# A hybrid decoder layer on one core: low parts of weights shared with GpSimd, recurrence products spread over four array quadrants

## The chip, the core and the metric

The kernel runs on one core of one Trainium2 chip. The metric is the device time of one execution in microseconds (us). Every engine named here belongs to that core: TensorE (PE in the profile; PEld is its weight load), VectorE (DVE), ScalarE (ACT), GpSimd (POOL) and SyncE (SP), whose queue issues most of the DMA transfers.

## What is computed

One layer of a decoder on 264 tokens at once: 256 tokens of a prompt and one new token for each of 8 other sequences. The model width is 2048. The parts are:

```python
x = x + 0.5 * swiglu(rmsnorm(x, n1), f1g, f1u, f1d)      # first FFN, inner width 5504
h = rmsnorm(x, nm)
proj = h @ w_in                                          # 2048 x 4864
# attention: 16 query heads, 4 key/value heads, window 128, sinks, relative bias
# RWKV-7 time mixing, 16 heads of 64x64 state:
#   S = S * exp(logw) + (S @ -kk) (kk * a)^T + v k^T ;  y = S @ r
x = x + concat(o_att, o_rwkv) @ w_out
x = x + 0.5 * swiglu(rmsnorm(x, n2), f2g, f2u, f2d)      # second FFN
```

All inputs and outputs are float32. The outputs are the final norm of x, new key/value windows, the recurrence's states and the last projected columns ("shift").

## The kernel before, in words

**Weights.** Every large product is made in three passes of a reduced float32 format (`F32R`). `chunk` (line 125) loads 128x512 weights into `raw` by a DMA on SP, ScalarE rounds them into `hi` (line 132), and another engine subtracts, `lo = raw - hi` (the helper `tt`, line 59). `gemm` (line 136) takes 16 such 128x128 blocks in chunks of four, and for each block issues three matmuls of 264 columns: `hi*xh`, `hi*xl`, `lo*xh`. There are 6 buffers of `raw` and 4 of `hi` and of `lo`, so that ScalarE can round at most about three chunks ahead of the one that TensorE reads. `chunk` runs with high priority: the scheduler may put it ahead of other work of its engines. The engine for `lo` is VectorE everywhere.

**Stages.** The first FFN, then `mixing_body` (w_in, attention, recurrence, w_out), then the second FFN. In the mixing stage `win(t)` (line 399) computes one of 38 tiles of 128 columns of `proj` (4 chunks, 48 matmuls): tiles 0 and 1 are the small projections, 2 to 25 belong to the eight pairs of recurrent heads (three tiles each), 26 to 29 to keys and values, 30 to 37 to queries. `SEQ` (line 39) has their order. After each chunk `gemm` calls `tick`, which advances every waiting task (a Python generator) to its next `yield`. So the small work of the recurrence and of attention lies between large matmuls, and `pause(n)` moves a step by n chunks. A list scheduler then writes the order of each engine, and each engine runs its order strictly.

**Recurrence.** The tasks take the head pairs in four batches of two. `prep` (one for each pair) builds, from the projected tiles, decays, keys and 64x64 matrices for four time blocks of 64 tokens (`c`); it ends with `gv` (line 524, products of `Gm` and `UV`) and `dps` (line 530, the eight other sequences' states times two vectors, 64x64 by 64x2). `chain` (one for each batch) reloads 32x32 blocks in another layout, runs a 30-step triangular solve on VectorE (lines 570 to 577, tiles `st` and `Xt`), completes the inverse `TT` with 32x32 products, and then makes, for both pairs and four blocks: `wus` (line 614, `TT` by two of the three parts of `KR`, 64x128), copies of it into `W` and `uv` by ScalarE and VectorE in turn (lines 622 and 626), `pbs` (lines 628 to 637: `W` by `BT` and `W` by `Gm`), `pN` and `pY`, and then three steps over `c` (line 660) that carry the state `S`: each multiplies `PT` by `S` into one bank and `S` by `KR` into `pY`. A 64x64 product reads one half of the 128 partitions (`HALF`) and writes one half. In all these products but `gv` the half written is the half read, so that the two heads of a pair use two of the four quadrants of TensorE's array.

After the last `prep`s the shift output `shc` is sent by a DMA on ScalarE's queue (line 887, right after the last batch is started); `shc` is filled by one small GpSimd copy for each tile (line 412). At the end of the last chain five transposes of `XD` (line 701) and ScalarE's copies (lines 703, 704) make `XR` for the states of the 8 other sequences, which are finished in the second FFN. Eight-column copies `y<-XD` stand on ScalarE (line 680).

Of the kernel before, what the change touches and what calls it, by code (L numbers as in the profile page):

```python
# [10 lines left out]
ALU = mybir.AluOpType  # L11
AX = mybir.AxisListType

P = 128
# [33 lines left out]
def body(tc, I, O):  # L48
# [51 lines left out]
    with ExitStack() as ctx:  # L100
# [24 lines left out]
        def chunk(src, n, e, ahead=True):  # L125
            w = n * P
            with tc.high_priority() if ahead else nullcontext():
                raw = wp.tile([P, CH * P], F32, tag="raw", bufs=NRAW, name=uid("raw"))
                hi = wp.tile([P, CH * P], F32R, tag="hi", bufs=NHL, name=uid("hi"))
                lo = wp.tile([P, CH * P], F32R, tag="lo", bufs=NHL, name=uid("lo"))  # L130
                SP.dma_start(raw[:, :w], src)
                A.copy(hi[:, :w], raw[:, :w])  # L132
                tt(e, lo[:, :w], raw[:, :w], hi[:, :w].bitcast(F32), ALU.subtract)
            return hi, lo

        def gemm(ps, src, xs, step=None, rng=None, ahead=True, ready=None):
            n = len(xs)
            for k0 in range(0, n, CH):
                k1 = min(n, k0 + CH)
                if rng and k0 not in rng:  # L140
                    continue
                hi, lo = ready or chunk(src[:, k0 * P:k1 * P], k1 - k0, V, ahead)
                for k in range(k0, k1):
                    xh, xl = xs[k]
                    c = slice((k - k0) * P, (k - k0 + 1) * P)
                    mm(ps[:, :T], hi[:, c], xh, k == 0, False)
                    mm(ps[:, :T], hi[:, c], xl, False, False)
                    big[0] = mm(ps[:, :T], lo[:, c], xh, False, k == n - 1)
                if step:
                    step()  # L150
# [206 lines left out]
        def mixing_body(mx, n2, n3, XD, XR):  # L357
# [68 lines left out]
            def prep(p, bt, k, xrr, xk, xv):  # L426
# [103 lines left out]
                dps = mp()  # L530
                for i in range(NB):
                    for h in range(2):
                        r = HALF[h]
                        mm(dps[r, 2 * i:2 * i + 2], st[i // 4][r, i % 4, :], XD[r, 6:8, p, i])
                dv = dps[:, 0:16].rearrange("p (b s) -> p s b", s=2)
                A.copy(XD[:, 0, p, :], dv[:, 0])
                tt(G, dq, dq, XD[:, 0:4:3, p, :], ALU.mult)
# [15 lines left out]
            def chain(bt):  # L553
# [53 lines left out]
                for h in range(2):  # L607
                    r = slice(h * 64, h * 64 + 32)
                    A.copy(TT[r, :, 32:64], ps[r, :n * P].rearrange("p (c t) -> p c t", t=32))
                yield  # L610
# [3 lines left out]
                wus = [mp() for _ in range(n)]  # L614
                for k in range(n):
                    for c in range(4):
                        for h in range(2):
                            r = HALF[h]
                            mm(wus[k][r, c * P:c * P + P], TT[r, k * 4 + c, :], bt.KR[k][r, 0:3:2, c, :])
                for k in range(n):  # L620
                    v = wus[k].rearrange("p (c t) -> p c t", c=4)
                    (A.copy, V.tensor_copy)[k % 2](W[:, k], v[:, 1:4, 0:64])
                for k in range(n):
                    v = wus[k].rearrange("p (c t) -> p c t", c=4)
                    for h in range(2):
                        (V.tensor_copy, A.copy)[h](uv[HALF[h], :, k, HALF[h]], v[HALF[h], :, 64:128])
                yield
                pbs = [mp() for _ in range(n)]
                for k in range(n):
                    for c in range(1, 4):  # L630
                        x = (c - 1) * P
# [3 lines left out]
                        for h in range(2):  # L635
                            r = HALF[h]
                            mm(pbs[k][r, x + 64:x + P], W[r, k, c - 1, :], bt.Gm[k][h][r, c, 64:128])
                for k in range(n):
                    v = pbs[k][:, :384].rearrange("p (c t) -> p c t", c=3)
                    A.copy(PT[:, k], v[:, :, 0:64])  # L640
                    tt(V, bt.KR[k][:, 1, 1:4, :], v[:, :, 64:128], bt.KR[k][:, 1, 1:4, :], ALU.add)
                pN, pY = mp(), mp()
                for k in range(n):
                    for c in range(4):
# [4 lines left out]
                for k in range(n):  # L649
                    for c in range(4):  # L650
                        x = (k * 4 + c) * 64
                        for h in range(2):
                            r = HALF[h]
                            mm(pY[r, x:x + 64], uv[:, c, k, r], bt.Gm[k][h][:, c, 64:128],
                               k + c == 0, c == 0, skip_group_check=True)
                tt(V, N, pN[:, :n * 256].rearrange("p (k c t) -> p k c t", k=n, c=4),
                   bc(wc[:, bt.p0:bt.p0 + n, :].unsqueeze(3), (P, n, 4, 64)), ALU.mult)
# [2 lines left out]
                for c in range(1, 4):  # L660
                    ps = mp()
                    for k in range(n):
                        for h in range(2):
                            r = HALF[h]
                            mm(ps[r, k * 64:k * 64 + 64], PT[r, k, c - 1, :], S[r, k])
                    for k in range(n):
                        for h in range(2):
                            r = HALF[h]
# [12 lines left out]
                for k in range(n):  # L681
                    A.dma_start(O["wkvp"][bt.p0 + k], S[:, k])
                g2s = [load(I["g2"][bt.p0 + k], (P, P)) for k in range(n)]
# [11 lines left out]
                    stt(o, o, vc(VLB + p), gp[:, :T], ALU.add, ALU.mult)  # L695
                    mixed[p] = o
                if len(bts) == nbat and bt is bts[-1]:
                    ps = mp()
                    xt = mp()
                    for i in range(5):  # L700
                        TE.transpose((ps, xt)[i > 3][0:64, i % 4 * P:i % 4 * P + P], XD[:, i, :, :], ident)
                    for h in range(2):
                        A.copy(XR[HALF[h], 0:4], ps[0:64].rearrange("p (c t) -> p c t", c=4)[:, :, HALF[h]])
                        A.copy(XR[HALF[h], 4], xt[0:64, HALF[h]])
                yield

            def gnorm(y):
# [169 lines left out]
            for kind, i in SEQ:  # L877
                if kind == "b":
# [4 lines left out]
                        spawn(prep(p, bt, k, *x))  # L883
                    bat.append(spawn(chain(bt)))
                    bts.append(bt)
                    if len(bat) == len(BATCH):
                        A.dma_start(O["sh"], shc)
# [43 lines left out]
            for pi, ks in enumerate(PASS):  # L931
# [182 lines left out]
```

## Time and profile before

| what | value |
|---|---|
| time, median of 3 runs | 1959.75 us (1958.75 to 1960.01) |
| the profiled execution | 1958.83 us |
| its span, first to last instruction | 1957.0 us |
| mean granted TensorE clock | 0.998 |
| mixing stage in that span | about 744 to 1192 us |

The profile is one execution as the hardware recorded it; 1.83 us of its time lie outside the span. Busy shares are of the span. A matmul's recorded duration overlaps with that of its neighbours, so for TensorE the distance between the starts of consecutive matmuls tells what one costs. A float32 product (not `F32R`) appears as two matmul records. In the timeline a row "x32" merges 32 instructions that follow each other.

### The profile page before, as it was taken

Reading aid. Unit: us, or ns where it says so; the run is one execution under the profiler, and the core shown is the slowest. Engines: PE = TensorE matmul, PEld = TensorE weight load, DVE = VectorE, ACT = ScalarE, POOL = GpSimd, SP = SyncE. Lnnn points to the kernel's source line nnn. Section 1 sums busy time; section 2 is a strip of 40 time slices with the busy share of each in tenths; the row PEclk is TensorE's granted clock in tenths of the full one; section 3 lists DMA queues with packets and bytes.
Section 4 is the critical chain, followed back from the end, with each engine's and each line's share of the span. In section 5 each row is a group of like instructions: output and inputs, shape, how many; then the busy total and the mean of one; then the engine's idle time right before and its main releaser. Section 6 shows DMA issues by size and latency. Waiting matters only on the chain.

```text
span 1957.0 us, 45229 instructions
## 1 busy us (share of the span) xinstructions
PE 1940.1 (99%) x17011; PEld 1922.1 (98%) x17011; DVE 1313.1 (67%) x2591; ACT 1036.4 (53%) x2069; POOL 264.1 (13%) x382
## 2 busy tenths in 40 slices
PE   9999999999999999999999999999999999999998
PEld 9999999999999999999889999999999999999998
DVE  5865555655556567799988766766666666666665
ACT  5644444444444456665556755654444444444445
POOL 0401001010010122232210000210101001010012
PEclk9999999999999999999999999999999999999999
DMA  7666666666656567555455455566666666666654
GB/s 241 178 194 194 186 194 196 184 189 178 188 183 185 184 194 230 165 162 153 136 151 167 137 157 185 176 187 188 191 189 193 188 194 191 191 195 183 195 182 148
DMA packets 218875, 357.26 MB, mean 183 GB/s; under 512 B 33552, under 2 KB 72352, under 8 KB 218656
## 3 DMA queue, kind: packets, MB, share of 16 engines
q1 hardware_dynamic: 212144, 345.76, 59.4%
q10 hardware_dynamic: 6512, 8.61, 1.4%
q8 instruction: 133, 2.18, 0.4%
q14 instruction: 86, 0.70, 0.1%
HBM read 346.67 MB, written 9.69 MB: 182 GB/s over the span
## 4 chain that ended last, share of the span: by engine, by line
PE 95%; DVE 3%; DMA 1%; issue 1%; ACT 1%; SPq 0%; DVEq 0%; POOL 0%; ACTq 0%
PE acc L75 87%; PE m L75 7%; DVE lo L59 1%; DVE Xt L59 0%; DVE st L59 0%; DMA Xt<-sa 0%; DMA x<-in_x 0%; DMA raw<-in_win 0%; DVE y L59 0%; SPq L564 0%; DVE gm L59 0%; ACT t L69 0%; DMA sa<-gm 0%; PE m L782 0%; ACT BT L521 0%
## 5 line engine op out<-in xcount | busy, mean ns | idle before, releaser
L59 DVE TENSOR_TENSOR lo<-raw,hi 128x512 fp32r<-128x512 f32 (+1 forms) x1288 | 874.5, 683 | 511.0 <-ACT hi L132 489.8
L132 ACT CAST hi<-raw 128x512 fp32r<-128x512 f32 (+1 forms) x1288 | 777.0, 606 | 822.0 <-PE acc L75 741.5
L75 PE MATMUL acc<-x,hi 128*128 128x264 f32 x5034 | 932.7, 286 | 2.2 <-DVE o L62 1.2
L75 PEld LDWEIGHTS acc<-x,hi 128*128 128x128 f32 x5034 | 781.4, 189 | 5.8 <-ACT hi L132 2.4
L75 PE MATMUL acc<-x,lo 128*128 128x264 f32 x2517 | 719.8, 286 | 0.5 <-DVE lo L59 0.5
L75 PE MATMUL acc<-h,hi 128*128 128x264 f32 x2752 | 495.0, 284 | 0.0
L75 PEld LDWEIGHTS acc<-x,lo 128*128 128x128 f32 x2517 | 475.5, 189 | 2.9 <-DVE lo L59 1.3
L75 PEld LDWEIGHTS acc<-h,hi 128*128 128x128 f32 x2752 | 424.4, 189 | 0.0
L75 PE MATMUL acc<-h,lo 128*128 128x264 f32 x1376 | 387.8, 284 | 0.0
L75 PEld LDWEIGHTS acc<-h,lo 128*128 128x128 f32 x1376 | 259.2, 189 | 0.0
L59 POOL TENSOR_TENSOR t<-t,t 128x264 f32<-128x264 f32 x74 | 80.3, 1085 | 1095.9 <-DVE t L59 949.7
L75 PE MATMUL acc<-y,hi 128*128 128x264 f32 x648 | 122.7, 284 | 0.0
L75 PE MATMUL acc<-o,hi 128*128 128x264 f32 x648 | 120.1, 284 | 0.0
L75 PE MATMUL acc<-kv,hi 128*128 128x264 f32 x582 | 109.2, 284 | 0.0
L75 PEld LDWEIGHTS acc<-y,hi 128*128 128x128 f32 x648 | 101.2, 189 | 0.1
L75 PEld LDWEIGHTS acc<-o,hi 128*128 128x128 f32 x648 | 100.1, 189 | 0.0
L62 DVE SCALAR_TENSOR_TENSOR x<-acc,x 128x264 f32<-128x264 f32 x192 | 81.2, 427 | 24.5 <-PE acc L75 23.6
L75 PE MATMUL acc<-y,lo 128*128 128x264 f32 x324 | 92.0, 284 | 0.0
L75 PE MATMUL acc<-o,lo 128*128 128x264 f32 x324 | 92.0, 284 | 0.0
L75 PEld LDWEIGHTS acc<-kv,hi 128*128 128x128 f32 x582 | 90.0, 189 | 0.0
L59 DVE TENSOR_TENSOR t<-acc,t 128x264 f32<-128x264 f32 x156 | 67.4, 432 | 32.8 <-PE acc L75 32.8
L75 PE MATMUL acc<-kv,lo 128*128 128x264 f32 x291 | 82.7, 284 | 0.0
(280 smaller groups left out, 1534.9 us busy)
## 6 DMA issues: line engine op xcount, KB each, us to landing
raw<-in_gu SPq DMA_DIRECT2D x688, 256.0 KB, 3.4
raw<-in_dn SPq DMA_DIRECT2D x224, 256.0 KB, 2.9
raw<-in_win SPq DMA_DIRECT2D x152, 256.0 KB, 3.4
raw<-in_dn SPq DMA_DIRECT2D x160, 192.0 KB, 2.7
raw<-in_wout SPq DMA_DIRECT2D x64, 256.0 KB, 3.3
xsp<-x ACTq DMA_DIRECT2D x16, 132.0 KB, 3.6
x<-xsp SPq DMA_DIRECT2D x16, 132.0 KB, 4.0
ld<-in_sT SPq DMA_DIRECT2D x16, 128.0 KB, 3.7
```

Source lines behind the costliest of these rows:

```text
L59: return e.tensor_tensor(out=out, in0=a, in1=b, op=op)
L62: return V.scalar_tensor_tensor(out=out, in0=a, scalar=s, in1=b, op0=op0, op1=op1)
L75: return TE.matmul(out, lhsT, rhs, start=start, stop=stop, **k)
L132: A.copy(hi[:, :w], raw[:, :w])
```

## The change

It has four parts.

1. In `win(t)` with t from 14 to 37 (24 tiles), every second chunk's `lo` is computed by GpSimd (`G`) and not by VectorE: 48 of 1128 such instructions.
2. The 64x64 products of the recurrence are placed so that one head's product writes the other half (`o`) where another product of the same head writes the same half (`r`): `TT` by `KR[2]` (64 columns, four blocks) goes to `ub[o]`, `TT` by `KR[0]` (64 columns, three blocks) to `wb[r]`; `W` by `BT` to `pb[o]`, `W` by `Gm` to `gb[r]`; `PT` by `S` stays at `r` and `S` by `KR` goes to `pY[o]`; `gv` and `dps` are issued in one loop. The copies swap the halves back.
3. The copies of these products stand on ScalarE (`W` one for both pairs, `uv`, `PT`, `y` by halves); the copies `y<-XD` stand on GpSimd and come earlier.
4. Order: one more chunk of `pause` ahead of the first batch's `TT` products (`LAG`), `pause(2)` for `yield` at two places of `chain`; the transposes into `XR` become a task of their own, started at the end of the last chain, three chunks later; the DMA of `shc` stands ahead of the second query tile; all tasks are drained before the mixing stage ends.

In the compiled order of each engine this gives 112 products `m<-kr,TT` of 64 columns for 64 of 128 columns, the other products in the same numbers; VectorE loses 48 `lo`, 4 `W` and 8 `uv`; GpSimd gains 48 `lo` and 8 `y<-XD`; ScalarE has two more table loads (18 for 16), the larger copies `W` (4 of 128x384 for 4 of 128x192), `PT` (8 of 64x384 for 8 of 128x192), `uv` (8 of 64x512 for 8 of 64x256) and `y` (16 of 64x256 for 8 of 128x256 and the 8 small ones).

```diff
+LAG = (8, 7, 7, 7)
+SHARE = 14
...
-                hi, lo = ready or chunk(src[:, k0 * P:k1 * P], k1 - k0, V, ahead)
+                hi, lo = ready or chunk(src[:, k0 * P:k1 * P], k1 - k0, G if share and k0 // CH % 2 else V, ahead)
...
-                gemm(ps, I["win"][t], n2.xs, tick)
+                gemm(ps, I["win"][t], n2.xs, tick, share=t >= SHARE)
...
-                gv = mp()
-                for c in range(4):
+                gv, dps = mp(), mp()
+                for i in range(NB):
+                    c, g = i // 2, i % 2
                     for h in range(2):
                         r, o = HALF[h], HALF[1 - h]
-                        mm(gv[r, c * 64:c * 64 + 64], bt.Gm[k][h][o, c, 0:64], bt.UV[o, c, k, r])
+                        mm(dps[r, 2 * i:2 * i + 2], st[i // 4][r, i % 4, :], XD[r, 6:8, p, i])
+                        if h == g:
+                            mm(gv[r, c * 64:c * 64 + 64], bt.Gm[k][h][o, c, 0:64], bt.UV[o, c, k, r])
...
-                yield from pause(7)
+                yield from pause(LAG[bt.i])
...
+                for k in range(n):
+                    G.tensor_copy(Ys[k][:, NP:T], XD[:, 7, bt.p0 + k, :])
...
-                            r = HALF[h]
-                            mm(wus[k][r, c * P:c * P + P], TT[r, k * 4 + c, :], bt.KR[k][r, 0:3:2, c, :])
+                            r, o = HALF[h], HALF[1 - h]
+                            mm(ub[o, x:x + 64], TT[r, k * 4 + c, :], bt.KR[k][r, 2, c, :])
+                            if c:
+                                mm(wb[r, x:x + 64], TT[r, k * 4 + c, :], bt.KR[k][r, 0, c, :])
...
+                A.copy(W, v[:, :, 1:4, :])
...
+                    A.copy(uv[HALF[h], :, :, HALF[h]], v[HALF[1 - h]])
+                yield from pause(2)
...
-                            mm(pbs[k][r, x:x + 64], W[r, k, c - 1, :], bt.BT[k][r, c, r])
-                        for h in range(2):
-                            r = HALF[h]
-                            mm(pbs[k][r, x + 64:x + P], W[r, k, c - 1, :], bt.Gm[k][h][r, c, 64:128])
+                            mm(pb[o, x:x + 64], W[r, k, c - 1, :], bt.BT[k][r, c, r])
+                            mm(gb[r, x:x + 64], W[r, k, c - 1, :], bt.Gm[k][h][r, c, 64:128])
...
                             mm(ps[r, k * 64:k * 64 + 64], PT[r, k, c - 1, :], S[r, k])
-                    for k in range(n):
-                        for h in range(2):
-                            r = HALF[h]
-                            x = (k * 4 + c) * 64
-                            mm(pY[r, x:x + 64], S[r, k], bt.KR[k][r, 1, c, :], False, True, skip_group_check=True)
+                            mm(pY[o, x:x + 64], S[r, k], bt.KR[k][r, 1, c, :], False, True, skip_group_check=True)
...
-                    A.copy(Ys[k][:, :NP], pY[:, k * NP:(k + 1) * NP])
-                    A.copy(Ys[k][:, NP:T], XD[:, 7, bt.p0 + k, :])
+                    for h in range(2):
+                        A.copy(Ys[k][HALF[h], :NP], pY[HALF[1 - h], k * NP:(k + 1) * NP])
...
+                    spawn(turned())
...
-                    if len(bat) == len(BATCH):
-                        A.dma_start(O["sh"], shc)
...
+                    if i == 1:
+                        A.dma_start(O["sh"], shc)
...
+            drain(list(tasks))
```

More of the change, by code (lines that the diff above doesn't have):

```diff
@@ L134, in chunk, with gemm @@
             return hi, lo
-        def gemm(ps, src, xs, step=None, rng=None, ahead=True, ready=None):
+        def gemm(ps, src, xs, step=None, rng=None, ahead=True, ready=None, share=False):
             n = len(xs)
@@ L609, in chain @@
                     A.copy(TT[r, :, 32:64], ps[r, :n * P].rearrange("p (c t) -> p c t", t=32))
-                yield
+                yield from pause(2)
                 Ys = [yb[bt.p0 + k] for k in range(n)]
+                for k in range(n):
+                    G.tensor_copy(Ys[k][:, NP:T], XD[:, 7, bt.p0 + k, :])
                 uv = bt.UV
                 N = ring((P, n, 4, 64), "N", 1)
-                wus = [mp() for _ in range(n)]
+                ub, wb = mp(), mp()
                 for k in range(n):
@@ L616, in chain @@
                     for c in range(4):
+                        x = (k * 4 + c) * 64
                         for h in range(2):
-                            r = HALF[h]
-                            mm(wus[k][r, c * P:c * P + P], TT[r, k * 4 + c, :], bt.KR[k][r, 0:3:2, c, :])
-                for k in range(n):
[L621 to L624, printed above, removed]
-                    for h in range(2):
-                        (V.tensor_copy, A.copy)[h](uv[HALF[h], :, k, HALF[h]], v[HALF[h], :, 64:128])
@@ L627, in chain @@
-                yield
-                pbs = [mp() for _ in range(n)]
+                            r, o = HALF[h], HALF[1 - h]
+                            mm(ub[o, x:x + 64], TT[r, k * 4 + c, :], bt.KR[k][r, 2, c, :])
+                            if c:
+                                mm(wb[r, x:x + 64], TT[r, k * 4 + c, :], bt.KR[k][r, 0, c, :])
+                v = wb[:, :n * 256].rearrange("p (k c t) -> p k c t", k=n, c=4)
+                A.copy(W, v[:, :, 1:4, :])
+                v = ub[:, :n * 256].rearrange("p (k c t) -> p c k t", k=n, c=4)
@@ L629, in chain @@
+                for h in range(2):
+                    A.copy(uv[HALF[h], :, :, HALF[h]], v[HALF[1 - h]])
+                yield from pause(2)
+                pb, gb = mp(), mp()
                 for k in range(n):
                     for c in range(1, 4):
-                        x = (c - 1) * P
+                        x = (k * 3 + c - 1) * 64
                         for h in range(2):
-                            r = HALF[h]
-                            mm(pbs[k][r, x:x + 64], W[r, k, c - 1, :], bt.BT[k][r, c, r])
@@ L635, in chain @@
-                        for h in range(2):
-                            r = HALF[h]
-                            mm(pbs[k][r, x + 64:x + P], W[r, k, c - 1, :], bt.Gm[k][h][r, c, 64:128])
+                            r, o = HALF[h], HALF[1 - h]
+                            mm(pb[o, x:x + 64], W[r, k, c - 1, :], bt.BT[k][r, c, r])
+                            mm(gb[r, x:x + 64], W[r, k, c - 1, :], bt.Gm[k][h][r, c, 64:128])
+                v = pb[:, :n * 192].rearrange("p (k c t) -> p k c t", k=n, c=3)
@@ L638, in chain @@
+                for h in range(2):
+                    A.copy(PT[HALF[h]], v[HALF[1 - h]])
+                v = gb[:, :n * 192].rearrange("p (k c t) -> p k c t", k=n, c=3)
                 for k in range(n):
-                    v = pbs[k][:, :384].rearrange("p (c t) -> p c t", c=3)
-                    A.copy(PT[:, k], v[:, :, 0:64])
-                    tt(V, bt.KR[k][:, 1, 1:4, :], v[:, :, 64:128], bt.KR[k][:, 1, 1:4, :], ALU.add)
+                    tt(V, bt.KR[k][:, 1, 1:4, :], v[:, k], bt.KR[k][:, 1, 1:4, :], ALU.add)
@@ L652, in chain @@
                         for h in range(2):
[L653 to L654 removed]
+                            mm(pY[HALF[1 - h], x:x + 64], uv[:, c, k, HALF[h]], bt.Gm[k][h][:, c, 64:128],
                                k + c == 0, c == 0, skip_group_check=True)
@@ L678, in chain @@
                 for k in range(n):
-                    A.copy(Ys[k][:, :NP], pY[:, k * NP:(k + 1) * NP])
-                    A.copy(Ys[k][:, NP:T], XD[:, 7, bt.p0 + k, :])
+                    for h in range(2):
+                        A.copy(Ys[k][HALF[h], :NP], pY[HALF[1 - h], k * NP:(k + 1) * NP])
                 for k in range(n):
@@ L697, in chain, with turned @@
                 if len(bts) == nbat and bt is bts[-1]:
[L698 to L704, printed above, removed]
+                    spawn(turned())
+                yield
+            def turned():
+                yield from pause(3)
+                ps, xt = mp(), mp()
+                for i in range(5):
+                    TE.transpose((ps, xt)[i > 3][0:64, i % 4 * P:i % 4 * P + P], XD[:, i, :, :], ident)
+                yield
+                for h in range(2):
+                    A.copy(XR[HALF[h], 0:4], ps[0:64].rearrange("p (c t) -> p c t", c=4)[:, :, HALF[h]])
+                    A.copy(XR[HALF[h], 4], xt[0:64, HALF[h]])
                 yield
```

9 lines of the change are left out of this document (2 added, 7 removed).

## The prediction, made before the result was known

> **What bounds the kernel now.** I read the page first: the busy shares, then the chain of work that ended last.
>
> ```profile
> span 1957.0 us, 45229 instructions
> ...
> PE 1940.1 (99%) x17011; PEld 1922.1 (98%) x17011; DVE 1313.1 (67%) x2591; ACT 1036.4 (53%) x2069; POOL 264.1 (13%) x382
> ...
> PE 95%; DVE 3%; DMA 1%; issue 1%; ACT 1%; SPq 0%; DVEq 0%; POOL 0%; ACTq 0%
> ```
>
> TensorE is the bound: 95% of the chain. Taking load from another engine gains nothing unless TensorE waits for that engine; making TensorE's own instructions fewer or shorter gains one for one. The change touches only the mixing stage, so I read the table of busy time in three stretches of it (columns: us, then busy us of PE, PEld, DVE, ACT, POOL with counts, granted clock, DMA share, GB/s).
>
> ```profile
> 744.00:900.00 156.00, 155.10 (x1597) 151.09 (x1596) 128.66 (x290) 102.37 (x251) 42.38 (x101) 1.00 0.61 178
> 900.00:1000.00 100.00, 96.92 (x1026) 91.98 (x1025) 93.35 (x265) 61.59 (x146) 20.64 (x47) 1.00 0.52 146
> 1000.00:1192.00 192.00, 189.82 (x1938) 182.07 (x1937) 140.23 (x412) 115.72 (x309) 13.73 (x33) 1.00 0.54 156
> ```
>
> TensorE is nearly always busy here too, at full clock. The reader should see the middle row: VectorE works 93.35 of 100 us and TensorE lacks 3.08 us. There two engines are at their limit together; in the other rows VectorE has a fifth or more to spare.
>
> **Part 1, the quadrants.** The chain in order of time gives the cost of a block of products (start, us, what):
>
> ```profile
> 883.64 2.30 PE acc L75 x19
> 885.94 1.89 PE m L75 x32
> ...
> 897.62 0.61 PE m L75 x16
> ```
>
> A large matmul takes 2.30/19 = 0.121 us. The 32 records at 885.94 are one batch's `TT` by `KR`, the 16 at 897.62 one step of the state. TensorE's timeline shows the pace within such blocks (start, us, what, count):
>
> ```profile
> 889.60 0.28 PE L75 MATMUL m<-gm,W 64*64 64x64 f32 x4
> 889.71 0.28 PE L75 MATMUL m<-BT,W 64*64 64x64 f32 x4
> ...
> 890.76 0.28 PE L75 MATMUL m<-gm,W 64*64 64x64 f32 x4
> ```
>
> Four records (two products, on two quadrants) start every (890.76 - 889.60)/10 = 0.116 us. The kernel before has one place where four quadrants work together, because the scheduler wove `gv` (which crosses halves) into `dps` (which doesn't):
>
> ```profile
> 823.03 0.51 PE L75 MATMUL m<-uv,gm 64*64 64x64 f32 x10
> ...
> 823.37 0.23 PE L75 MATMUL m<-uv,gm 64*64 64x64 f32 x2
> 823.40 0.20 PE L75 MATMUL m<-XD,ld 64*64 64x2 f32 x2
> 823.43 0.23 PE L75 MATMUL m<-uv,gm 64*64 64x64 f32 x2
> ...
> 823.49 0.22 PE L75 MATMUL m<-uv,gm 64*64 64x64 f32 x2
> ...
> 824.55 0.90 PE L75 MATMUL m<-XD,ld 64*64 64x2 f32 x26
> 825.38 0.39 PE L75 MATMUL acc<-x,hi 128*128 128x264 f32 x1
> ```
>
> From 823.37 to 823.49 eight records start in 0.12 us: the second pair of quadrants costs nothing. So I price four quadrants at eight records in 0.116 us. For one batch:
> - `TT` by `KR`: 32 records of 128 columns took 1.89. Now each quadrant pair has at most 8 pairs of products of 64 columns, 8 x 0.116 = 0.93, plus 0.15 that a block needs to start (0.61 less four steps of 0.116 at 897.62). Saved 0.8.
> - `W` by `BT` and `Gm`: 48 records, 12 x 0.116 = 1.39, halved. Saved 0.7.
> - three steps of the state: 4 x 0.116 = 0.46 each, halved. Saved 0.7.
> - `gv` and `dps`: 825.38 - 823.03 = 2.35 for 96 records. The 64 of `dps` now set the pace, 16 x 0.116 = 1.86 plus 0.15. Saved 0.3.
>
> Together 2.5 a batch, **10.1 us** in four (3.2 + 2.8 + 2.8 + 1.3), all on TensorE's path. What this row cannot show is four quadrants all streaming 64 columns, since `dps` streams 2. Bounds: 3 to 11 us.
>
> **Part 2, waits that go.** Three rows of TensorE, two of ScalarE, and a group with its idle time:
>
> ```profile
> 954.55 2.35 PE L75 MATMUL m<-kr,TT 64*64 64x128 f32 x32 [1.46 <-ACT TT L609]
> ...
> 1101.28 0.30 PE L701 MATMUL m<-C,XD 128*64 128x128 f32 x1 [0.40 <-ACT XR L703]
> 1101.80 0.39 PE L75 MATMUL acc<-x,hi 128*128 128x264 f32 x1 [0.22 <-DVE x L59]
> ```
>
> ```profile
> 953.75 0.35 ACTq L887 DMA_DIRECT2D out_sh<-shc  x1
> 954.14 0.75 ACT L609 COPY TT<-m 32x256 f32<-32x256 f32 x2 [3.83 <-POOL shc L412]
> ```
>
> ```profile
> L75 PE MATMUL m<-BT,W 64*64 64x64 f32 x96 | 6.3, 225 | 1.3 <-DVE W L622 1.3
> ```
>
> The shift output's DMA stood on ScalarE's queue behind a GpSimd copy; ScalarE was idle 3.83 us, and TensorE waited 1.46. Ahead of the second query tile every `shc` copy is long done, so this goes. The transposes into `XR` stopped TensorE for 0.40 + 0.22; as a task of their own they have no successor that hurries. Saved **2.1 us**. The 1.3 us for VectorE's copy `W` get a longer ScalarE copy in exchange: taken as 0, between 0 and 1.3 gained.
>
> **Part 3, ScalarE's extra work**, as groups of the mixing stage:
>
> ```profile
> L132 ACT CAST hi<-raw 128x512 fp32r<-128x512 f32 x214 | 131.1, 618 | 102.5 <-PE acc L75 82.1 <-DVE Xt L59 3.7 <-ACT t L414 3.4
> ```
>
> ```profile
> L69 ACT ACT_TABLE_LOAD x10 | 12.8, 1283 | 0.2
> ```
>
> Two more table loads are 2.6 us and the larger copies some 5, on an engine busy 62% in the fullest stretch. What hides them: `hi` runs three chunks ahead of TensorE, 36 x 0.121 = 4.4 us. In the compiled order three loads stand between two `hi` casts in the first batch's norm (3 x 1.28 and some 1.6 of activations, 5.4 us), but five small blocks of TensorE lie there too. Cost 0; up to 1 us if that cover fails. The 8 small copies `y<-XD` that leave ScalarE hide likewise.
>
> **Part 4, low parts on GpSimd.** This is the disputed part. What one costs is not in the trace; the nearest rows are its products of 264 and of 16 columns:
>
> ```profile
> L59 POOL TENSOR_TENSOR o<-o 128x264 f32<-128x264 f32 x4 | 3.0, 757 | 7.9 <-ACT o L69 7.9
> ...
> L59 POOL TENSOR_TENSOR t<-t,XD 128x16 f32<-128x16 f32 x8 | 1.9, 232 | 19.0 <-ACT XD L536 19.0
> ```
>
> (757 - 232)/248 = 2.1 ns a column, so 512 columns take 757 + 248 x 2.1 = 1.28 us: an estimate, for 0.68 us on VectorE below. And the two engines hold each other up:
>
> ```profile
> 77.90 0.88 POOL L59 TENSOR_TENSOR t<-t,t 128x264 f32<-128x264 f32 x1 [2.10 <-DVE t L59]
> 78.08 1.24 DVE L59 TENSOR_TENSOR lo<-raw,hi 128x512 fp32r<-128x512 f32 x1
> ```
>
> ```profile
> 888.98 2.54 POOL L59 TENSOR_TENSOR t<-XD 128x16 f32<-128x16 f32 x1
> ```
>
> VectorE's `lo` took 1.24 us beside a GpSimd product that had begun before it, and ended 0.54 after that product; a 16-column product of GpSimd took 2.54 instead of 0.23 while VectorE ran one SBUF instruction after another. VectorE's groups from 900 to 1000 us:
>
> ```profile
> L59 DVE TENSOR_TENSOR lo<-raw,hi 128x512 fp32r<-128x512 f32 x46 | 31.2, 680 | 2.3 <-ACT hi L132 1.5 <-PE acc L75 0.5
> ...
> L59 DVE TENSOR_TENSOR Xt<-Xt,st 128x60 f32<-128x60 f32 (+23 forms) x58 | 12.0, 207 | 1.0
> L59 DVE TENSOR_TENSOR st<-X,Xt 128x60 f32<-128x60 f32 (+23 forms) x58 | 11.6, 200 | 2.5 <-DMA Xt<-sa 1.7
> ```
>
> These three, all with two SBUF inputs, are 54.8 of its 93.35 us; with smaller such groups about two thirds. In this stretch 23 of 46 low parts leave: 23 x 0.68 = 15.6 us. They come back as blocked time of 23 x 1.28 x 2/3 = 19.6. VectorE then needs 97.4 us, while TensorE would need 100 - 3.0 (one batch's savings and some of its neighbours') - 1.5 (the wait) = 95.5. With VectorE's present idle share the stretch lasts 97.4/0.9335 = 104.3, with none 97.4. I take the middle, 100.8: a cost of **5.2 us**, between 1.9 and 8.8. Elsewhere VectorE has room: 0.
>
> **Sum.** 1958.83 - 10.1 - 2.1 + 5.2 = 1951.8 against the profiled execution. The median of the runs shown is 0.92 higher, so I predict **1952.7 us**, with 1947 to 1957 for this case alone.
>
> **Rivals** (all with the 0.9 added).
> - *Sharing is free.* GpSimd finds its gaps, VectorE is really relieved, and the 1.3 us before `BT` go: 1958.8 - 10.1 - 2.1 - 1.3 + 0.9 = 1946.2. For it: GpSimd is busy only 20.64 of 100 us. Against it: the 2.54 us row.
> - *Low parts come late.* In the strict order of GpSimd a low part waits as the product at 888.98 did, 2.3 us: 0.62 for `hi`, 2.3, 1.28 and some 0.5 for a small instruction ahead make 4.7, against the 4.4 us after which TensorE is back at the buffer. 0.3 us for half of 48 is 7 more: 1959.9. For it: only three chunks of cover. Against it: the small products between them lengthen that cover.
> - *VectorE becomes the bound*, the slower side. Place: 900 to 1000 us. If each low part on GpSimd blocks VectorE for its whole 1.28 us, VectorE needs 93.35 - 15.6 + 29.4 = 107.2, the stretch lasts 107.2/0.9335 = 114.8, a cost of 19.3: 1966.8. It decides from 0.99 us blocked per low part (a stretch of 107.7 us, which eats the whole 12.2). For it: the 1.24 us row. Against it: a third of VectorE's work reads PSUM. The Trainium skill (SBUF — State Buffer, Who interferes with whom) has the rule: VectorE with two SBUF inputs and GpSimd reading SBUF exclude each other for a whole instruction, and one with a PSUM input doesn't take part. By that rule the trace agrees, with 1.24 us for 0.68.
> - *Four quadrants pay less*: a record may cost some least time of its own. The smallest products of the kernel stream 32 columns:
>
> ```profile
> 882.31 0.69 PE L75 MATMUL m<-TT,W 32*32 32x32 f32 x32
> 882.93 0.71 PE L75 MATMUL m<-t,C 128*128 128x264 f32 x2
> ```
>
> (882.93 - 882.31)/32 = 19.4 ns a record. With this as a floor, `TT` by `KR` (56 records of 64 columns in the new form) takes 1.09 + 0.15 and saves 0.65, `W` by `BT` takes 0.93 and saves 0.46, the steps take 0.31 each and save 0.46, and `gv` with `dps` keeps its 0.3: 1.87 a batch, 7.5 us. The sum is 1958.8 - 7.5 - 2.1 + 5.2 + 0.9 = 1955.3. For it: that row. Against it: 15 ns a record at 823.37. The Trainium skill (TensorEngine Tiling (Array Packing), Instruction Overhead) says "Each matmul has ~60 cycle overhead on TRN2"; at 2.4 GHz that is 25 ns, an estimate by that page, which would leave some 0.7 us a batch saved and give 1960; the trace has 15 and 19 ns instead, and it decides.
>
> **How the numbers follow.** Chances: forecast 0.47, free 0.17, late 0.15, VectorE bound 0.13, quadrants paying less 0.08. A measurement of this kernel tells about 0.2% (3.9 us) from no change. Below 1955.8: 0.43 of the forecast's, all of free, 0.03 of late, 0.04 of quadrants: 0.67 faster. Above 1963.7: 0.10 of VectorE's case and 0.03 of late: 0.13 slower. The rest, 0.20, is the same. The range 1945 to 1962 leaves out most of the VectorE case and the edge of the free one, and holds the bounds of the unknown costs otherwise.
>
> **What would show it.** Right: blocks of `TT` by `KR` last 1.1 us, steps of the state about 0.4; no ScalarE wait for `shc`; GpSimd low parts of 1.3 to 1.9 us; VectorE still over 90% busy in the dense stretch. Wrong: TensorE waiting for a GpSimd `lo` for more than 6 us in all, records of the four-quadrant blocks 25 ns apart, or a dense stretch with VectorE clearly under 85% (then sharing was free).

## The result, and the profile after

The changed kernel takes **1970.07 us** (median of 4 runs, 1969.49 to 1971.20) against 1959.88 for the kernel before in the same comparison: a ratio of 1.0053, with a 95% interval from 1.0036 to 1.0071. It is slower by some 10 us, where 7 us faster was forecast. The page of its profiled execution begins:

```profile
span 1968.4 us, 45438 instructions
...
PE 1938.4 (98%) x17107; PEld 1918.9 (97%) x17107; DVE 1315.4 (67%) x2531; ACT 1043.4 (53%) x2071; POOL 316.1 (16%) x438
```

The span grew by 11.4 us, VectorE's busy time by 2.3 (though 48 low parts left it), GpSimd's by 52. The three stretches of the mixing stage again (columns as before; the third last is the granted clock):

```profile
744.00:900.00 156.00, 152.78 (x1584) 147.53 (x1583) 127.81 (x266) 101.63 (x246) 51.59 (x117) 0.99 0.58 175
900.00:1000.00 100.00, 93.28 (x1043) 88.00 (x1042) 90.83 (x224) 63.20 (x146) 44.19 (x69) 0.98 0.49 138
1000.00:1192.00 192.00, 183.29 (x1940) 175.63 (x1939) 139.19 (x404) 117.25 (x309) 33.22 (x51) 0.97 0.52 152
```

TensorE now stands still for 18.65 us of these 448 instead of 6.16, and the clock, 1.00 in all three rows before, is lower in each. (The changed kernel is behind by then, so the same row holds somewhat less of its work.) What was to get shorter did. TensorE's timeline, one batch's `TT` by `KR`:

```profile
888.88 1.15 PE L77 MATMUL m<-kr,TT 64*64 64x64 f32 x56
889.97 0.39 PE L77 MATMUL acc<-x,lo 128*128 128x264 f32 x1
```

889.97 - 888.88 = 1.09 us for 1.89. The 48 records of `W` by `BT` and `Gm` take 0.86 us for 1.54, a step of the state mostly 0.39 for 0.61 (from start to the start of what follows). To see where the time went, I lay the traces side by side by work: from the start of the 6481st large matmul (`acc`) to that of the 8161st, which is 822.8 to 1154.7 us before and 822.9 to 1165.7 after. Outside this stretch the traces differ by 0.4 us, 0.3 of it after the last large matmul. Inside it I split TensorE's time: stalls are what a distance between two starts has beyond 0.12 us (0.10 after a small product), where the distance is over 0.42; "half clock" is the time lost in spells with a granted clock of 0.50; the rest is work and small gaps.

| kernel | stretch, us | stalls | half clock | rest |
|---|---|---|---|---|
| before | 331.8 | 7.4 | 0 | 324.4 |
| changed | 342.7 | 20.6 | 8.5 | 313.6 |

The rest is **10.8 us shorter**, much as the forecast's 10.1 for the quadrants; **stalls and half clock take 21.7 back**. This split, and every one below, is of one execution. The view of TensorE's waits from 855 to 1100 us names what it stood for (engine, what, total, times, longest):

```profile
PE m L77 <- DVE st L61: 4.7, 1, 4.7
PE m L77 <- ACT t L71: 4.1, 3, 2.2
PE m L511 <- ACT t L487: 2.1, 1, 2.1
PE m L511 <- DVE gm L61: 1.9, 1, 1.9
...
PE acc L77 <- POOL lo L61: 0.6, 1, 0.6
```

TensorE hardly ever waits for a GpSimd low part (0.6 us), and no longer for `TT` behind the shift output or for `XR`. It waits for VectorE's steps and for ScalarE's small steps of the recurrence. What a low part on GpSimd does is in the groups of GpSimd and VectorE, 744 to 1200 us, first of the changed kernel (GpSimd, then VectorE), last VectorE's of the kernel before:

```profile
L61 POOL TENSOR_TENSOR lo<-raw,hi 128x512 fp32r<-128x512 f32 x48 | 63.5, 1324 | 72.3 <-ACT hi L134 49.0 <-PE acc L77 8.2 <-PE m L77 4.5
```

```profile
L61 DVE TENSOR_TENSOR Xt<-Xt,st 128x60 f32<-128x60 f32 (+10 forms) x120 | 35.8, 298 | 2.8 <-DVE st L61 0.2
L61 DVE TENSOR_TENSOR st<-X,Xt 128x60 f32<-128x60 f32 (+10 forms) x120 | 35.3, 294 | 9.9 <-DMA Xt<-sa 7.5
```

```profile
L59 DVE TENSOR_TENSOR Xt<-Xt,st 128x60 f32<-128x60 f32 (+10 forms) x120 | 24.6, 205 | 2.3
L59 DVE TENSOR_TENSOR st<-X,Xt 128x60 f32<-128x60 f32 (+10 forms) x120 | 24.5, 204 | 4.7 <-DMA Xt<-sa 2.9
```

A low part takes 1.32 us (1.28 forecast). VectorE's 240 solve steps took 0.205 us each before and take 0.296 now: 22 us more, of the 48 x 0.68 = 32.6 that VectorE was to be spared. One collision in the timeline of all engines:

```profile
867.22 1.27 POOL L61 TENSOR_TENSOR lo<-raw,hi 128x512 fp32r<-128x512 f32 x1 [2.69 <-ACT hi L134]
867.33 1.25 DVE L61 TENSOR_TENSOR st<-X,Xt 128x65 f32<-128x65 f32 x1
...
868.87 0.22 DVE L61 TENSOR_TENSOR st<-X,Xt 128x60 f32<-128x60 f32 x1
...
869.26 0.68 DVE L61 TENSOR_TENSOR gm<-m,C 128x512 f32<-128x512 f32 x1
...
870.00 0.44 PE L511 MATMUL m<-C,kr 128*128 128x128 f32 x2 [1.88 <-DVE gm L61]
```

A step of 0.22 us in the other batches takes 1.25 here and ends 0.09 us after the low part; the mask product `gm` behind it is a microsecond late, and TensorE stands 1.88 us. What follows is in the table of busy time (first pair: around this stall; second pair: around one of 2.3 us):

```profile
867.50:870.90 3.40, 1.52 (x12) 1.27 (x13) 3.30 (x8) 2.62 (x10) 0.99 (x1) 1.00 0.21 58
870.90:874.30 3.40, 3.40 (x42) 3.16 (x40) 3.12 (x13) 2.35 (x7) 0.00 (x0) 0.50 0.17 26
...
915.30:918.70 3.40, 2.33 (x18) 2.05 (x16) 3.37 (x7) 3.34 (x6) 0.20 (x1) 1.00 0.56 145
918.70:922.10 3.40, 2.29 (x17) 2.23 (x18) 2.57 (x6) 2.45 (x5) 1.30 (x1) 1.00 0.23 75
```

After 3.4 us with TensorE busy for 1.52, the clock is halved for the next 3.4, a loss of 1.7. The second stall is no shorter, but falls across two such stretches (2.33 and 2.29 busy), and costs nothing further. All spells of this trace begin on one grid of 3.41 us (870.9, 939.2, 1034.7, 1082.5), and last one or two of its steps. Three of them, 6.8 us of loss, follow stalls of 2.1, 2.3 and 4.9 us. The last, 1.7 us, follows no stall over 0.6: TensorE was busy for 3.08 of the 3.40 us before it, 1.95 of them with products of 8 columns. The table of busy time there, and TensorE's timeline:

```profile
1079.10:1082.50 3.40, 3.08 (x51) 2.81 (x47) 2.18 (x8) 3.35 (x14) 1.16 (x3) 1.00 0.52 168
1082.50:1085.90 3.40, 3.11 (x28) 3.02 (x29) 2.08 (x9) 1.60 (x6) 0.00 (x0) 0.50 0.27 81
```

```profile
1080.00 1.95 PE L77 MATMUL m<-qb,ld 128*128 128x8 f32 x16
```

### The profile page after: what moved, and what is told of

It is laid out like the page before. It is cut to its first block, busy times and chain, and to the rows that moved or that the text cites. A ratio compares the mean times of both kernels' runs of the same rounds, so it can differ in the third digit from the quotient of the medians.

```text
span 1968.4 us, 45438 instructions
## 1 busy us (share of the span) xinstructions
PE 1938.4 (98%) x17107; PEld 1918.9 (97%) x17107; DVE 1315.4 (67%) x2531; ACT 1043.4 (53%) x2071; POOL 316.1 (16%) x438
## 4 chain that ended last, share of the span: by engine, by line
PE 48%; DVE 3%; ACT 1%; DMA 1%; issue 0%; SPq 0%; DVEq 0%; ACTq 0%
PE acc L77 44%; PE m L77 3%; DVE st L61 1%; DVE Xt L61 1%; DVE lo L61 1%; ACT t L71 0%; DVE y L61 0%; DVE gm L61 0%; DMA sa<-gm 0%; ACT hi L134 0%; DVE t L720 0%; SPq L564 0%; DVE t L61 0%; DMA raw<-in_win 0%; DMA raw<-in_wout 0%
## 5 line engine op out<-in xcount | busy, mean ns | idle before, releaser
L61 DVE TENSOR_TENSOR lo<-raw,hi 128x512 fp32r<-128x512 f32 x1240 | 843.7, 684 | 514.0 <-ACT hi L134 491.3
```

The lines of the kernel that those rows point to most:

```text
L61: return e.tensor_tensor(out=out, in0=a, in1=b, op=op)
```

## Experiments

Three theories to begin with. **L**: GpSimd's reading holds VectorE up, and TensorE's products come late. **O**: the scheduler, counting on a relieved VectorE, packs TensorE's order too tightly. **C**: the other parts of the change make the waits.

**no_share**: the changed kernel without GpSimd low parts.

```diff
-SHARE = 14
+SHARE = 38
```


> The changed kernel without its GpSimd low parts; everything else stays. Theory L (each GpSimd low part holds VectorE up for about 1 us, and what TensorE waits for comes late) and theory O (the order planned with low parts on GpSimd is too tight for TensorE, whatever GpSimd does) both expect the waits to go: 1958.8 - 10.3 (shorter blocks) - 2 (waits) gives 1945 to 1950 us, stalls of TensorE over 0.3 us between 744 and 1160 us at most 6 us in all, clock 0.998. Theory C (ScalarE's larger copies and the moved steps make the waits) expects 1962 to 1972 us with most of the 20.6 us of stalls still there.

**1965.06 us, 1.0024** [1.0013, 1.0035]. So the low parts on GpSimd cost some 5 us (1970.07 less 1965.06), and half of the loss is elsewhere: L and O fail by 15 us, C is right for that half.

**share_only**: the kernel before with the low parts alone (the diff's lines of `SHARE`, `gemm` and `win`).


> The kernel before with 48 low parts on GpSimd and nothing else of the change. L and O expect the same loss as in the changed kernel, 13 us of waits and 8.5 us of half clock, on top of the old blocks: 1972 to 1985 us. C expects 1957 to 1963 us.

**1975.43 us, 1.0080** [1.0065, 1.0095]: 15 us for the low parts alone, as L and O said. The parts don't add up: with the low parts on GpSimd in place, the rest of the change gains 5.4 us (1975.43 to 1970.07); without them it loses 4.4 (1960.65 to 1965.06). Why the low parts cost 15 us alone and 5 beside the rest, no run explains.

**left_out**: the changed kernel; the shared chunks have no low part, `lo` is `hi`. It leaves out a part of the computation and serves for its time alone.

```diff
+                if e is G:
+                    return hi, hi
                 tt(e, lo[:, :w], raw[:, :w], hi[:, :w].bitcast(F32), ALU.subtract)
```


> The changed kernel, in which the 48 low parts are not computed by any engine: TensorE multiplies the rounded weights in their place, so the low weights of these chunks are missing from the result. VectorE is relieved of 48 x 0.68 us as the change meant, and no GpSimd instruction holds it. L expects 1940 to 1949 us, with hardly a stall over 1 us. O expects stalls as in the changed kernel, since the planner again believes VectorE to be free: 1955 to 1970 us. C expects 1962 to 1972 us.

**1952.16 us, 0.9961** [0.9946, 0.9976]. O falls: with the same belief in a relieved VectorE, and nothing on GpSimd, it is 18 us faster than the changed kernel. L is 3 us off its range too: one stall of 4.8 us stayed, with 3.4 us of half clock.

**twice**: all low parts on VectorE, and the 48 once more on GpSimd.

```diff
+                tt(V, lo[:, :w], raw[:, :w], hi[:, :w].bitcast(F32), ALU.subtract)
+                if e is G:
+                    tt(G, twin, raw[:, :w], hi[:, :w].bitcast(F32), ALU.subtract)
```


> The changed kernel with all low parts on VectorE, and the same 48 subtractions done by GpSimd a second time into a tile that nobody reads. VectorE isn't relieved and is held up. L expects more than the changed kernel, 1968 to 1990 us, with the solve's steps again some 0.3 us in the mean. O expects it near the kernel without GpSimd low parts, 1946 to 1953 us.

**1992.43 us, 1.0164** [1.0149, 1.0179]: 27 us over no_share, for results that nobody reads. L again, 2 us beyond its range.

**writes** takes the rival within L away, that GpSimd's own small products come late behind the large ones: GpSimd is as busy, but only writes.

```diff
-                    tt(G, twin, raw[:, :w], hi[:, :w].bitcast(F32), ALU.subtract)
+                    for j in range(3):
+                        i = G.memset(twin[:, :400], 0.0)
+                        tc.add_manual_dep(i.ins, cast.ins.name, mybir.DependencyInfo(mybir.DependencyClass.Sync, mybir.DependencyReason.DATA))
```


> The kernel twice, in which GpSimd, in place of the 48 subtractions that nobody reads, writes zeros into the same tile, three instructions of 400 columns for each, about 1.3 us together, waiting for the same ScalarE rounding. GpSimd is as busy and its small products are as late, but it reads no SBUF. If VectorE is held up by GpSimd's reading: 1963 to 1972 us, the solve's steps back at 0.20 us in the mean. If GpSimd's own small products come late behind the large ones: 1985 to 1996 us, as twice.

**1965.19 us, 1.0024** [1.0014, 1.0034]: as no_share. The groups, GpSimd and VectorE, first of twice, then of writes:

```profile
L61 POOL TENSOR_TENSOR twin<-raw,hi 128x512 fp32r<-128x512 f32 x48 | 72.6, 1512 | 59.3 <-issue 43.3 <-ACT hi L134 12.7 <-POOL XD L61 1.3
L61 DVE TENSOR_TENSOR st<-X,Xt 128x60 f32<-128x60 f32 (+10 forms) x120 | 35.6, 296 | 8.4 <-DMA Xt<-sa 6.2
```

```profile
L138 POOL MEMSET twin<- 128x400 f32 x144 | 62.2, 432 | 69.8 <-ACT hi L134 58.2 <-ACT t L492 6.2
L61 DVE TENSOR_TENSOR st<-X,Xt 128x60 f32<-128x60 f32 (+10 forms) x120 | 24.7, 206 | 9.7 <-DMA Xt<-sa 7.4
```

62 us of GpSimd writing leave VectorE's steps at 206 ns; 73 us of reading make them 296. It is the reading that costs. The Trainium skill (SBUF — State Buffer, Who interferes with whom) says the same: VectorE with two SBUF inputs contends with a GpSimd instruction that reads SBUF, not with one that only writes.

Now the other half. **V**: VectorE, by what it has to do in its strict order, sets when the recurrence's products can run, so TensorE's savings come back as waits. **Q**: the quadrants pay their 10 us, and the moved steps or ScalarE's copies cost them.

**two_quads**: no_share with the products into `ub`, `pb` and `pY` back in their own half (`gv` and `dps` stay in one loop), all else kept.

```diff
-                            mm(ub[o, x:x + 64], TT[r, k * 4 + c, :], bt.KR[k][r, 2, c, :])
+                            mm(ub[r, x:x + 64], TT[r, k * 4 + c, :], bt.KR[k][r, 2, c, :])
```
(the same for `pb` and `pY`, and the copies without the swap)


> The kernel no_share (1965.1 us, span 1961.3) with its products back on two quadrants, so that only the placement goes and all copies and steps stay. Theory V: VectorE sets the pace between 850 and 1040 us, and what TensorE saves there comes back as waiting; so the shorter blocks were worth little, and this runs in 1964 to 1969 us, with fewer and shorter stalls than the 18.3 us of no_share. Theory Q: the shorter blocks do pay their 10 us and the moved steps or ScalarE's copies cost them: 1972 to 1977 us.

**1963.47 us, 1.0016** [1.0007, 1.0026], not slower than no_share. Four quadrants are worth nothing here: Q falls. V's range is missed by half a microsecond, on the fast side.

**left_out_two**: the same edit on left_out.


> The kernel left_out (1952.2 us; the 48 low parts computed by no engine) with its products back on two quadrants. With VectorE's low parts the placement was worth nothing (no_share 1965.1, two_quads 1963.5). Theory V (VectorE sets the pace in the dense stretch): with VectorE relieved the placement pays, 1958 to 1963 us here. If the placement never pays, whatever VectorE does: 1950 to 1954 us.

**1959.42 us, 0.9998** [0.9989, 1.0008], 7 us over left_out. The four corners, with the stretch of the traces split as above:

| kernel | us | stretch | stalls | half clock | rest |
|---|---|---|---|---|---|
| two_quads | 1963.5 | 335.8 | 10.5 | 3.4 | 321.9 |
| no_share (four) | 1965.1 | 336.1 | 18.3 | 6.8 | 311.0 |
| left_out_two | 1959.4 | 331.6 | 7.3 | 3.4 | 320.9 |
| left_out (four) | 1952.2 | 323.8 | 9.4 | 3.4 | 311.0 |

Four quadrants shorten TensorE's work by 10 to 11 us in both rows. With VectorE's 48 low parts in the way it is given back in full, 7.8 as stalls and 3.4 as half clock; without them 2.1 is given back. V holds for this, with one reservation: the scheduler wrote a new order for each of the four, so a corner's stalls belong to its order as well as to VectorE's load. What the placement is worth with the low parts on GpSimd was not measured. One such stall in no_share, VectorE and then TensorE:

```profile
1018.09 0.19 DVE L61 TENSOR_TENSOR st<-X,Xt 128x30 f32<-128x30 f32 x1 [5.08 <-DMA Xt<-sa]
```

```profile
1033.27 0.34 PE L77 MATMUL m<-N,PT 64*64 64x64 f32 x1 [4.60 <-DVE st L61]
```

VectorE stands 5.08 us for the reload of the last batch's `Xt`, while the `N` of the batch before stands behind the solve in its order; TensorE stands 4.60 for that `N`. But VectorE is not simply full: it is busy for 171.53 of the 200 us from 850 to 1050 there.

**left_out_before**: the same low parts left out of the kernel before.


> The kernel before, in which the same 48 low parts are computed by no engine (TensorE multiplies the rounded weights in their place); TensorE's work is unchanged. Theory V: VectorE already held TensorE back in the kernel before, so this removes most of its 7.4 us of stalls: 1950 to 1954 us. Theory Q: VectorE is not what is waited for, 1957 to 1961 us.

**1958.31 us, 0.9987** [0.9977, 0.9996]. V's number is missed by 4 us and Q's is met. By the trace the stalls fell from 7.4 to 3.7 us, as V said, but two spells of half clock (3.4) took the gain, one of them with TensorE busy all through. That relieving VectorE pays little while TensorE's own work is the longer one is a guess from this pair.

**order_only**: the kernel before with all the moved steps, **order_undone**: no_share without them.

```diff
-                yield from pause(7)
+                yield from pause(LAG[bt.i])
...
-                yield
+                yield from pause(2)
```
(with `turned`, the shift DMA and the small copies as in the change)


> The kernel before with the order edits alone. The prediction's step said 2.1 us of waits go: 1957 to 1959 us. If the order edits make new waits: 1963 to 1972 us. Theory V: 1957 to 1962, since a chunk more of pause changes nothing in what VectorE has to do.

> The kernel no_share with the order edits undone (LAG 7 for all, one yield for pause(2), transposes inline, shift DMA and the small copies where they were); four quadrants and ScalarE's copies stay. If the order edits made the waits: 1946 to 1952 us. Theory V: 1957 to 1965 us, with stalls of 10 us or more in all. If ScalarE's copies made them: as no_share, 1962 to 1967.

**order_only 1965.05 us, 1.0030** [1.0019, 1.0042]; **order_undone 1963.88, 1.0017** [1.0008, 1.0026]. Alone the moved steps cost 4 to 6 us, which V didn't expect (1957 to 1962); beside the quadrants, undoing them wins nothing that can be told. Nor does a cost of ScalarE's copies show: two_quads has them on top of the moved steps and is no slower than order_only.

**moved_steps** has the shift DMA, `turned` and the draining alone, **pauses** the longer pauses and the early small copies alone, **quads_moved** is no_share with the pauses as before.


> The kernel before with the shift DMA ahead of the second query tile and the transposes into XR as a task of their own, nothing else. The prediction's part 2 gave 2.1 us for it: 1957 to 1959 us. If these steps make the new waits of order_only (1965.1): 1962 to 1967 us.

> The kernel before with the longer pauses (LAG 8 for the first batch, pause(2) at two places) and the early small copies on GpSimd, nothing else. The prediction gave them no cost: 1958 to 1961 us. If the pauses make the new waits of order_only: 1962 to 1968 us.

> The kernel no_share with the pauses as before, and only the shift DMA and the transposes moved; four quadrants and ScalarE's copies stay. If the pauses were what cost: 1950 to 1957 us, a version that beats both kernels. Theory V: 1960 to 1966 us, as no_share and order_undone.

**moved_steps 1962.85 us, 1.0016** [1.0006, 1.0026]; **pauses 1966.17, 1.0031** [1.0019, 1.0043]; **quads_moved 1963.70, 1.0019** [1.0009, 1.0028]. The pauses, with the early small copies, cost what order_only costs (stalls 11.5 us, half clock 6.8; order_only 11.6 and 5.1). But quads_moved doesn't win without them, as it should have if they alone were what cost. moved_steps ran between 1958.97 and 1966.63; in its profiled execution, the slowest of these, stalls are 8.3 and the rest 321.8, so the work is shorter than before and 8.5 us of half clock make the loss (the last section has the greater part of it). VectorE and TensorE in pauses:

```profile
1022.35 0.19 DVE L60 TENSOR_TENSOR st<-X,Xt 128x30 f32<-128x30 f32 x1 [7.01 <-DMA Xt<-sa]
1022.48 0.69 DVE L60 TENSOR_TENSOR lo<-raw,hi 128x512 fp32r<-128x512 f32 x1
```

```profile
1023.23 0.59 PE L76 MATMUL acc<-x,lo 128*128 128x264 f32 x1 [3.13 <-DVE lo L60]
```

It is the same reload. In the kernel before VectorE waited 1.20 us for it; here 7.01, with a low part behind it that TensorE needs. The changed kernel has it too, ahead of the 4.7 us for which TensorE stood:

```profile
1022.20 0.19 DVE L61 TENSOR_TENSOR st<-X,Xt 128x30 f32<-128x30 f32 x1 [7.49 <-DMA Xt<-sa]
```

That a longer pause elsewhere brings this about through the scheduler's order is argued, not shown.

**later_solve**, **later_solve_after**, **later_solve_before** are for theory **W**, that VectorE's wait for this reload is what costs: they were to put the last batch's solve later, in no_share, the changed kernel and the kernel before.

```diff
-DWAIT = (11, 11, 11, 3)
+DWAIT = (11, 11, 11, 8)
```


> The kernel no_share with the last batch's solve put 8 chunks after its reload is issued and not 3 (the last number of DWAIT). Theory W: the lost 10 us are waits of VectorE in its strict order: it stood 5.1 us idle at 1013 to 1018 us for the reload of Xt from memory, then worked through 60 solve steps ahead of the N that TensorE stood 4.9 us for, and the half clock after that cost up to 3.4 more. Then most of 4.9 + 3.4 goes: 1954 to 1959 us. If the wait is only moved (the solve is then late for the chain behind it): 1962 to 1968 us.

> The changed kernel with the same single number changed. Theory W: its 5.0 us stall at 1031 us and 3.4 us of half clock go, 1960 to 1965 us. If only moved: 1967 to 1973 us.

> The kernel before with the same single number changed. It had no such stall (VectorE waited 1.2 us for that reload and TensorE not at all), so theory W expects no gain: 1958 to 1964 us. It is the control for the other two.

**1964.89 us, 1.0026** [1.0016, 1.0037]; **1973.60, 1.0068** [1.0052, 1.0085]; **1961.03, 1.0007** [0.9997, 1.0017]: no gain. But these tell nothing of theory W, as the traces show: VectorE's first solve step stayed in its place, ahead of that `N`. At 20 chunks it does move behind it: **solve_20** (no_share) and **solve_20_after** (the changed kernel).


> The kernel no_share with the last batch's solve put 20 chunks after its reload is issued, so that the N of the batch before stands ahead of the first solve step on VectorE. Theory W: the 4.9 us stall for N goes, and with it 1.7 to 3.4 us of half clock: 1957 to 1961 us. If the last batch, now late, is what the output product waits for: 1965 us or more, with TensorE waiting after 1100 us.

> The changed kernel with the same number at 20. Theory W: the 5.0 us stall for N goes and some half clock: 1961 to 1966 us. If the late last batch is waited for: 1970 us or more.

**solve_20 1961.66 us, 1.0003** [0.9994, 1.0012]; **solve_20_after 1965.97, 1.0030** [1.0019, 1.0040]. Theory W holds for that part of the loss: the stall for `N` is gone from both traces, and they are 3.4 and 4.1 us faster (solve_20 is 0.7 us above W's range, solve_20_after just inside). solve_20 stands level with the kernel before; stalls came up later (1.3 and 1.7 us at 1127 to 1131, at half clock), smaller than the rival's, and the 4.7 us one at 991 us, for a VectorE step `o`, stayed. No version that keeps the whole computation beat the kernel before.

## Why the prediction was wrong

- **"all on TensorE's path"**, part 1: this step failed. The size was right (10.1 forecast, 10 to 11 measured as shorter work, the blocks at 1.09 us where 1.1 was forecast), the conclusion wrong: two_quads against no_share gives nothing for it. I read 95% of the chain on TensorE as "one for one". But the middle row of the stretches said that VectorE lacked only 6.65 us of 100 there; I used this to price the low parts, and not to ask whether a shorter TensorE would only wait for the same VectorE steps.
- **Part 2, waits that go**, 2.1 us: both waits went, as forecast. But I costed the longer pauses at nothing, without naming what would be late next, and this step failed too: the moved steps alone cost 4 to 6 us (order_only). In the traces of pauses and of the changed kernel the reload of `Xt` was late. One path through the runs shows how the forecast's 7 us of gain became 10 of loss: 1960.7 before, 1965.05 with the moved steps, 1965.06 with quadrants and copies as well, 1970.07 with the low parts on GpSimd.
- **Part 3, ScalarE's extra work**, 0 us: no run shows a cost (two_quads against order_only).
- **Part 4, low parts on GpSimd**, 5.2 us (the middle taken gives 100.8 - 95.5 = 5.3): 5 us by no_share, but 15 by share_only, so that the match in size is in part luck. The price of one (1.28 forecast, 1.32) and the lock were right too; VectorE's busy time in the middle row fell only from 93.35 to 90.83. "A third of VectorE's work reads PSUM" was too much: in the middle row it is some 23 us of 93, and much of the rest of that third are instructions with one input. The mechanism was half right: VectorE doesn't run out of time; in the collision shown, a solve step and what stands behind it come a microsecond late.
- **The clock** had no step in the sum. It cost 8.5 us, 6.8 of them behind three stalls and 1.7 behind none. In the mixing stage of the trace before no stall was over 1.7 us and the clock stood at 1.00; only the last 7 us of that span, with TensorE idle, were at 0.50. So the price of a stall wasn't to be read there.
- **Rivals.** "Sharing is free" and "low parts come late" (0.6 us waited) fell. "VectorE becomes the bound" came nearest, 1966.8 against 1970.07, and has the right engine; but it kept the 12.2 us of savings and put the whole loss on the low parts, so its number is near by luck. "Four quadrants pay less" fell as a price: 48 records of `W` by `BT` and `Gm` in 0.86 us are 17.9 ns each with the start of the block, less than its floor of 19.4 without.
- **My markers** (block lengths, no `shc` wait, low parts of 1.3 us, VectorE over 90% in the dense stretch) all came out right, and the total wrong. None of them looked at TensorE's idle time, where a saving is given back.

## What to carry to other kernels

Before counting a saving on the bound engine one for one, look for the engine next to it in that stretch: if its strict order holds what the bound engine needs next, the saving turns into waits. Work given to GpSimd that reads SBUF may come back to VectorE where VectorE runs instructions with two SBUF inputs: here 22 of 32.6 us did, in longer solve steps alone. And a stall may have half clock behind it: here three of 2.1 us and more cost 1.7 to 3.4 us on top, and one of 2.3 nothing.

## What the runs showed of the hardware

- **Half clock after idle time.** The Trainium skill (TensorE: Matmul & The Clock Gate, HAM oscillation — how this bites in real kernels) gives the rule as "no PE-idle gaps >~3.4µs". The spells of 3.41 us on a fixed grid agree with that page of the Trainium skill; here 1.88 us of idle time within one step of the grid was enough (1.52 of 3.40 busy), and the measurement decides. Busy time doesn't draw the line by itself: in no_share a step with 1.54 busy (990.2 to 993.6 us) was followed by full clock, in two_quads one with 2.53 (1013.15 to 1016.55) by half.
- **Small products may count as idle.** In moved_steps the clock fell with no stall ahead of it. TensorE's busy time and clock, and then what filled the first of these stretches:

```profile
1143.20:1146.60 3.40, 3.40 (x31) 3.35 (x30) 2.20 (x8) 0.88 (x3) 0.00 (x0) 1.00 0.72 216
1146.60:1156.80 10.20, 10.20 (x47) 9.84 (x47) 2.39 (x8) 2.91 (x10) 1.13 (x3) 0.50 0.15 46
```

```profile
1143.76 2.29 PE L75 MATMUL m<-sd,ld 128*128 128x8 f32 x20
```

  Busy all through, but for 2.3 us with products of 8 columns; half clock for 10.2 us. The spells at 1082.5 us in the changed kernel and at 1072.5 in left_out_before, one step each, both follow 16 products `m<-qb,ld` of 8 columns in 1.95 us. The trace before has both kinds of product at full clock. That it depends on how they fall on the grid is a guess.
- **Much of the spread of the runs goes with it.** In the comparison of two_quads the kernel before ranged from 1957.2 us to 1963.1; its 7 runs at a mean clock of 0.998 took 1958.9 us in the mean, its 3 at 0.995 took 1962.9. (0.003 of 1960 is 5.9 us.) Runs at one and the same mean clock still differ by some 3 us, so a difference of that size between two single executions says nothing.
